# The store of the decoded sequences' value rows: two transfers (112 and 15 partitions) in place of one with 127

## The chip, the cores and the metric

The kernel runs on one core of a Trainium2 chip, as one launch. Its time is the device time of that launch in microseconds. A run of the same program differs from the next by about 1 us.

## What is computed

One decoder layer for 256 prompt tokens and 8 decoded sequences of one token each (264 columns in all). Cut to what matters:

```python
def trunk_layer(x, pe, prm, cache):
    z = rms_norm(x, prm['g_pre_mix']) @ prm['w_in']          # q, k, v and the state-space input u
    attn, k_new, v_new = attn_prompt(...) or attn_sample(..., k_buf, v_buf)
    ssm, s_re, s_im = ssm_mix(u, prm, s0)
    merged = concat([rms_norm(attn, ...), rms_norm(ssm, ...)])
    x = x + rms_norm(merged @ prm['w_out'], ...)
    f = (silu(gu[..., :D_FF]) * gu[..., D_FF:]) @ prm['w_down']    # gu = rms_norm(x) @ w_gate_up
    x = x + rms_norm(f, ...)
    x = x + sigmoid(x @ prm['w_ple_gate']) * (pe @ prm['w_ple_proj'])

def attn_sample(q, k, v, sinks, k_buf, v_buf):
    vals = jnp.concatenate([v_buf, v], axis=1)               # 128 cached rows and the new one
    ...
    return out, keys[:, -WINDOW:], vals[:, -WINDOW:]
```

The last line is the one at hand: for each of the 8 decoded sequences the value cache is given back moved on by one row, that is, the cached rows 1 to 127 and the new row.

## The kernel before

All weights pass TensorE as one stream of blocks (128x128, with 264 columns on the other side). Eight blocks make a unit of 512 KB, which one transfer brings (`raw`, `w_load`, line 332; four buffers). After the first six units, each unit is split into a rounded part by ScalarE (`wh`, `w_high`, line 348) and a rest by VectorE (`wl`, `w_low`, line 356), and TensorE makes three products per block (`acc`, 24 matmuls in a unit). The phases of the stream are `in` (q, k, v, u), `oa` and `os` (the output projection for attention and for the state-space group), `gu`, `dn`, `pg` and `pp`. A unit's buffer can be loaded again once VectorE has made the rest of the unit four before it.

Between the blocks of phase `in`, TensorE also does the attention (`attn`, line 543: scores `s`, transposes `pt`, output `o`) and the state-space group (`ssm_x`: `px`, `ph`, with the table `xtab` that a transfer brings and VectorE's `X` made from it; `ssm_w`: `pw`; `ssm_y`: `py`, then `gy` on ScalarE and its transposes). Each engine works through its instructions in the order in which the program lists them.

That order is not written by hand. `Pace` (line 76) takes each piece of work as a generator and lists the pieces by a rough clock per engine; for a transfer that clock counts half a microsecond on SP, then the bytes (`move`, line 96). What is listed on one engine after another therefore depends on how many transfers there are.

All transfers are issued on SP, one after the other (`dma`, line 289). The value rows' stores stand in `epi_v` (line 505), behind the pieces of VectorE, TensorE and ScalarE on the v columns. The tile `vcd` holds the cached rows: partition r is row r, with 8 sequences of 128 floats (512 bytes) each. The store reads partitions 1 to 127 and writes, for each, 8 runs of 512 bytes that lie 64 KB apart:

```python
        dma(a["o_v"], vnat[:, 1, :])
        dma(a["o_vd"].rearrange("n r d -> r n d")[0:127], vcd[1:128, :, :])
        dma(a["o_vd"][:, 127, :], vself)
        pace.sig("v_out", "sp")
```

`v_out` is waited for in one place, by TensorE's stream on entering phase `os` (line 1529).

Of the kernel before, what the change touches and what calls it, by code (L numbers as in the profile page):

```python
# [16 lines left out]
P = 128  # L17
# [24 lines left out]
def stream_plan():  # L42
    """The order in which the blocks (matrix, output chunk, contraction chunk) pass the tensor engine.
    Eight in a row are a unit, which one transfer brings."""
    b = []

    def chunks(name, ms, nk):
        for m in ms:
            b.extend((name, m, k) for k in range(nk))

    def together(name, ms, nk):
        for k in range(nk):
            b.extend((name, m, k) for m in ms)

    together("in", [0, 4], 16)
    chunks("in", [1, 5, 2, 6, 3, 7, 8, 9] + list(range(10, 18)), 16)
    chunks("oa", range(16), 8)
    chunks("os", range(16), 8)
    chunks("pp", range(8), 2)
    together("gu", EARLY["gu"], 16)  # L60
    chunks("gu", [m for f in range(3, KF) for m in (f, KF + f) if m not in EARLY["gu"]], 16)
    chunks("dn", range(16), KF)
    chunks("pp", range(8, 16), 2)
    together("pg", EARLY["pg"], 16)
    chunks("pg", [m for m in range(16) if m not in EARLY["pg"]], 16)
    return [b[i:i + 8] for i in range(0, len(b), 8)]


# the jobs that share their contraction chunks at the start of these phases
# [6 lines left out]
class Pace:  # L76
    """Writes the program in about the order in which the engines get to it. A task is a generator whose
    segments (an engine, the events that it waits for, the buffers that it takes) are emitted at the
    earliest time that a rough clock per engine allows, the most urgent first."""
# [3 lines left out]
    def __init__(self):  # L83
        self.t = {"pe": 0.0, "dve": 0.0, "act": 0.0, "pool": 0.0, "sp": 0.0}
        self.link = 0.0
        self.table = None
        self.ev = {}
        self.tasks = []
        # when each of the free buffers of a kind came free
        self.res = {n: [0.0] * c for n, c in RES.items()}  # L90
        self.cur = "pe"
# [4 lines left out]
    def move(self, nbytes):  # L96
        """A transfer: the descriptors, then the link."""
        self.t["sp"] += 0.5
        self.link = max(self.link, self.t["sp"] + 0.65) + nbytes / 350e3
# [54 lines left out]
def places(ap):  # L154
    """The elements of a partition that an access touches."""
    i = np.array([ap.offset])
    for stride, n in ap.ap[1:]:
        i = (i[:, None] + stride * np.arange(n)[None]).reshape(-1)
    return i


def interleave(ops, issue=0.1, latency=0.13):
    """An order of the operations (call, operands; the first is written) in which one rarely waits for another."""
    writer, readers, deps = {}, {}, []
    for n, (_, args) in enumerate(ops):
        aps = [x for x in args if hasattr(x, "tensor")]
        d = set()
        for k, ap in enumerate(aps):
            t = ap.tensor.name
            w = writer.setdefault(t, np.full(2048, -1))  # L170
            i = places(ap)
            d.update(w[i].tolist())
            if k == 0:
                for m, j in readers.get(t, []):
                    if np.intersect1d(i, j).size:
                        d.add(m)
        for k, ap in enumerate(aps):
            if k:
                readers.setdefault(ap.tensor.name, []).append((n, places(ap)))
        writer[aps[0].tensor.name][places(aps[0])] = n  # L180
        deps.append(d - {-1, n})
    tail = [0.0] * len(ops)
    for n in reversed(range(len(ops))):
        for m in deps[n]:
            tail[m] = max(tail[m], tail[n] + issue + latency)
    order, end, t = [], {}, 0.0
    left = set(range(len(ops)))
    while left:
        ready = [(max([t] + [end[m] + latency for m in deps[n]]), -tail[n], n) for n in left if deps[n] <= end.keys()]
        t, _, n = min(ready)  # L190
        t += issue
        end[n] = t
        left.remove(n)
        order.append(ops[n][0])
    return order


def build(nc, tc, ctx, a):
# [11 lines left out]
    def deferred(f):  # L210
        """f, or while a list is kept, its call put on the list."""
        def g(*args):
            if later:
                later[-1].append((lambda: f(*args), args))
            else:
                f(*args)
        return g
# [111 lines left out]
    raws, highs, lows = {}, {}, {}  # L329
    at = {"unit": 0}  # L330
# [34 lines left out]
    def warm(func):  # L365
        """Brings an activation function's table in before it is needed."""
        act(spare, epst, func)

# [1 line left out]
    def rstd(ssqs, ones, out, name, evs=()):  # L370
        """out = 1/sqrt(mean + eps) for each column, on every partition; a task's segments. The sum of
        squares comes in one tile or in two, the second of which waits for evs."""
# [25 lines left out]
    def prep_x():  # L398
        """x, and x times the norm's gain."""
        xt = big.tile([P, KD, T], F32, tag="X3", name="xt")  # L400
        XF["t"] = xt
        xr = big.tile([P, KD, T], F32, tag="X1", name="xr")
        XF["r"] = xr
        cuts = [0, 2, 4, 7, 10, 13, 16]
        for c, (k0, k1) in enumerate(zip(cuts, cuts[1:])):
            yield "sp", [f"iss{c - 1}"] if 0 < c < NRAW else []
            dma(xr[:, k0:k1, :], a["x"][:, k0:k1, :])
            pace.sig(f"xl{k0}", "sp")
            if c == 0:
                dma(gains, a["gains"])  # L410
                pace.sig("c_g", "sp")
            for k in range(k0, k1):
                pace.ev[f"xl{k}"] = pace.ev[f"xl{k0}"]
# [91 lines left out]
    def epi_v(ps):  # L505
# [17 lines left out]
        dma(a["o_vd"].rearrange("n r d -> r n d")[0:127], vcd[1:128, :, :])  # L523
# [19 lines left out]
    def attn(g):  # L543
        """Both heads (kv, g): two blocks of queries."""
# [166 lines left out]
    # the imaginary parts, and at last what the products need of the tables: for al -(re + im) and im - re,  # L711
    # for fw, whose conjugate it is that counts, re - im and -(re + im)
# [29 lines left out]
    def exp_poly(out, x):  # L742
        """exp by range reduction and a polynomial."""
# [15 lines left out]
    def cmul(ore, oim, are, aim, bre, bim, t):  # L759
        """(are + i aim)(bre + i bim); t: four scratch tiles."""  # L760
# [7 lines left out]
    def ssm_setup():  # L768
# [69 lines left out]
        # fw[r] = a^(8-r), al[j] = a^(7-j) f  # L838
        n = 1
# [43 lines left out]
        while n < 32:  # L883
            # [0:n] known with n >= 1, the angle of step n in (pc, psn)
# [20 lines left out]
        # the decoded sequences' states, one step on, and their place in SB2  # L905
# [15 lines left out]
    def minus():  # L921
        """The table of sines with its sign turned."""
# [14 lines left out]
    def outer(o, tre, tab, b, bs, e):  # L937
        """o = table (over j) times b (over channels), as complex numbers, from three products."""
# [9 lines left out]
    def ssm_x(e):  # L948
# [43 lines left out]
        # the block's products over time: row (j, c') of step 7 - r is row (j + r, c') of the last step  # L992
# [79 lines left out]
    def ssm_side(e):  # L1072
        """The scan's factors, and the decoded sequences' states."""
# [47 lines left out]
    def ssm_glu(c, first):  # L1121
# [19 lines left out]
        # twice the gated value: (1 + tanh(z / 2)) times the other half  # L1141
# [232 lines left out]
    def epi_pg(ps, m):  # L1374
# [3 lines left out]
        # the last one in two parts, so that the one's way out overlaps the other's arithmetic  # L1378
# [36 lines left out]
    with ExitStack() as order:  # L1415
# [4 lines left out]
        # the tensor engine's clock rises after some microseconds of work: begin before the data is here  # L1420
# [33 lines left out]
        def enter(name):  # L1454
# [6 lines left out]
            if name == "os":  # L1461
                # from here on the program's own order
# [50 lines left out]
        def stream():  # L1513
            phase = None
            for ui, unit in enumerate(UNITS):
                at["unit"] = ui
                if ui == ACCU and ACC0 > 2:
                    # banks for the other work on this engine
# [3 lines left out]
                if unit[0][0] != phase:  # L1522
                    phase = unit[0][0]
                    if phase in ("os", "gu"):
                        # more banks for the stream
# [58 lines left out]
def _constants():  # L1584
# [8 lines left out]
    # rows of the decoded sequences' scores: 32 for a sequence, 16 of them heads  # L1593
# [10 lines left out]
    # the queries' factors: 1/8, and the score's slope put aside  # L1604
# [6 lines left out]
def _layout(x):  # L1611
    """The arrays of setup_inputs() in the layouts that the program loads."""
# [11 lines left out]
    # channel orders: attention chunk g holds (kv, d) of heads (0, g) and (1, g); a chunk of the  # L1624
    # state-space group holds (channel, group)
# [23 lines left out]
    # states: partition (half of the groups, state), free (ri, group of the half)  # L1649
# [10 lines left out]
    def eighths(v):  # L1660
        """[P, ri, groups, n] as [eighth, P, ri groups n]"""
# [66 lines left out]
```

## Time and profile before

| what | value |
|---|---|
| time, median of 3 runs | 1220.92 us (1220.55 to 1221.59) |
| span of the profiled execution | 1217.8 us (its own time is not listed; the runs lie 2.8 to 3.8 us above the span) |
| TensorE (PE) busy | 1181.8 us, 97% of the span |
| VectorE (DVE) busy | 750.6 us, 62% |
| ScalarE (ACT) busy | 590.0 us, 48% |
| GpSimd (POOL) busy | 55.0 us, 5% |
| longest single wait of TensorE | 20.0 us |

Times in the profile are microseconds from the start of the span. A timeline row gives the start, the length, the engine, the program's line, the operation and its tiles, and in brackets how long the engine had stood idle just before and what ended that. PEclk is the clock granted to TensorE as a share of its higher level: 1.00 is 2.4 GHz and 0.50 is 1.2 GHz. SPq is SP's queue, on which transfers are issued; its length is the time that the issuing takes, not that of the transfer.

### The profile page before, as it was taken

Reading aid. Unit: us, or ns where it says so; the run is one execution under the profiler, and the core shown is the slowest. Engines: PE = TensorE matmul, PEld = TensorE weight load, DVE = VectorE, ACT = ScalarE, POOL = GpSimd, SP = SyncE. Lnnn points to the kernel's source line nnn. Section 1 sums busy time; section 2 is a strip of 40 time slices with the busy share of each in tenths; the row PEclk is TensorE's granted clock in tenths of the full one; section 3 lists DMA queues with packets and bytes.
Section 4 is the critical chain, followed back from the end, with each engine's and each line's share of the span. In section 5 each row is a group of like instructions: output and inputs, shape, how many; then the busy total and the mean of one; then the engine's idle time right before and its main releaser. Section 6 shows DMA issues by size and latency. Waiting matters only on the chain.

```text
span 1217.8 us, 23880 instructions
## 1 busy us (share of the span) xinstructions
PE 1181.8 (97%) x9699; PEld 1153.7 (95%) x9699; DVE 750.6 (62%) x1325; ACT 590.0 (48%) x913; POOL 55.0 (5%) x97
## 2 busy tenths in 40 slices
PE   8993999999999999999999999999999999999998
PEld 7893887899999999999999999999999999999998
DVE  8992788967898555555555555555444444446864
ACT  6442887745575444443444444434343444335542
POOL 1111323210000000000000000000000000000000
PEclk9997999999999999999999999999999999999999
DMA  8863554467676666565656555555765666656773
GB/s 269 242 220 112 152 152 154 113 182 254 184 245 201 196 176 188 177 185 179 187 176 188 177 188 176 186 179 186 248 186 177 180 184 177 187 175 194 225 247 117
DMA packets 102184, 228.96 MB, mean 188 GB/s; under 512 B 26969, under 2 KB 50489, under 8 KB 101561
## 3 DMA queue, kind: packets, MB, share of 16 engines
q1 hardware_dynamic: 102073, 227.43, 60.7%
q8 instruction: 76, 1.25, 0.4%
q14 instruction: 35, 0.29, 0.1%
HBM read 214.60 MB, written 12.80 MB: 187 GB/s over the span
## 4 chain that ended last, share of the span: by engine, by line
PE 88%; DVE 6%; DMA 3%; ACT 1%; issue 1%; POOL 0%; SPq 0%; DVEq 0%
PE acc L283 82%; DMA raw<-in_w 2%; PE py L283 1%; DVE wl L222 1%; DVE X L222 1%; DVE rt L222 1%; PE pw L283 1%; PE pt L287 1%; PE s L283 1%; DVE sc L222 0%; ACT s L279 0%; DMA xtab<-in_xtab 0%; DMA xr<-in_x 0%; DVE xl L222 0%; DVE ssq_x L222 0%
## 5 line engine op out<-in xcount | busy, mean ns | idle before, releaser
L222 DVE TENSOR_TENSOR wl<-raw,wh 128x1024 fp32r<-128x1024 f32 x362 | 442.8, 1223 | 321.7 <-PE acc L283 246.8
L279 ACT ACTIVATE wh<-raw 128x1024 fp32r<-128x1024 f32 x362 | 383.9, 1061 | 459.5 <-PE acc L283 432.7
L283 PE MATMUL acc<-hh,wh 128*128 128x264 f32 x1408 | 399.6, 284 | 0.5 <-DVE n_t L236 0.5
L283 PE MATMUL acc<-hh,wl 128*128 128x264 f32 x1408 | 398.6, 283 | 0.0
L283 PE MATMUL acc<-hl,wh 128*128 128x264 f32 x1408 | 398.3, 283 | 0.1
L283 PEld LDWEIGHTS acc<-hh,wh 128*128 128x128 f32 x1408 | 265.2, 188 | 0.7 <-issue 0.7
L283 PEld LDWEIGHTS acc<-hl,wh 128*128 128x128 f32 x1408 | 265.0, 188 | 0.4 <-DVE hl L236 0.3
L283 PEld LDWEIGHTS acc<-hh,wl 128*128 128x128 f32 x1408 | 264.0, 188 | 0.0
L283 PE MATMUL acc<-f,wh 128*128 128x264 f32 x1408 | 256.8, 284 | 0.0
L283 PEld LDWEIGHTS acc<-f,wh 128*128 128x128 f32 x1408 | 217.8, 188 | 0.1
L283 PE MATMUL acc<-f,wl 128*128 128x264 f32 x704 | 199.7, 284 | 0.0
L283 PEld LDWEIGHTS acc<-f,wl 128*128 128x128 f32 x704 | 132.5, 188 | 0.0
L283 PE MATMUL acc<-x2h,wh 128*128 128x264 f32 x256 | 72.7, 285 | 0.0
L283 PE MATMUL acc<-x2h,wl 128*128 128x264 f32 x256 | 72.5, 284 | 0.0
L283 PE MATMUL acc<-xh,wh 128*128 128x264 f32 x240 | 72.1, 300 | 0.0
L283 PE MATMUL acc<-x2l,wh 128*128 128x264 f32 x256 | 71.8, 284 | 0.0
L283 PE MATMUL acc<-xl,wh 128*128 128x264 f32 x240 | 69.7, 290 | 0.4 <-DVE xl L222 0.4
L283 PE MATMUL acc<-xh,wl 128*128 128x264 f32 x240 | 69.3, 289 | 0.7 <-DVE wl L222 0.7
L222 DVE TENSOR_TENSOR uu<-acc,Rf 128x264 f32<-128x264 f32 x44 | 19.0, 432 | 51.0 <-PE acc L283 51.0
L283 PE MATMUL acc<-aops,wh 128*128 128x264 f32 x256 | 48.2, 289 | 0.0
L283 PEld LDWEIGHTS acc<-x2h,wh 128*128 128x128 f32 x256 | 48.1, 188 | 0.0
L283 PEld LDWEIGHTS acc<-x2h,wl 128*128 128x128 f32 x256 | 48.1, 188 | 0.0
(324 smaller groups left out, 1356.1 us busy)
## 6 DMA issues: line engine op xcount, KB each, us to landing
raw<-in_w SPq DMA_DIRECT2D x367, 512.0 KB, 3.6
T<-td SPq DMA_DIRECT2D x8, 512.0 KB, 4.3
xs<-in_x SPq DMA_DIRECT2D x2, 1056.0 KB, 9.4
ppd<-ppt SPq DMA_DIRECT2D x16, 132.0 KB, 3.6
x1d<-oo SPq DMA_DIRECT2D x4, 528.0 KB, 5.6
x<-x1d SPq DMA_DIRECT2D x2, 1056.0 KB, 7.9
ppr<-ppd SPq DMA_DIRECT2D x16, 132.0 KB, 3.7
xtab<-in_xtab SPq DMA_DIRECT2D x8, 256.0 KB, 3.6
```

Of the source, the lines that this page charges most:

```text
L222: V.tensor_tensor(out=out, in0=in0, in1=in1, op=op)
L279: S.activation(out=out, in_=in_, func=func, **kw)
L283: PE.matmul(out, lhsT, rhs, start=start, stop=stop)
L287: PE.transpose(out, in_, ident)
```

## The change

The store of 127 partitions is made as two, of 112 and of 15 partitions, one right after the other in the source. Together they write the same bytes to the same places. Comments are also taken out of the file, so that the lines below the store carry numbers that are higher by three.

```diff
         dma(a["o_v"], vnat[:, 1, :])
-        dma(a["o_vd"].rearrange("n r d -> r n d")[0:127], vcd[1:128, :, :])
+
+        ovd = a["o_vd"].rearrange("n r d -> r n d")
+        dma(ovd[0:112], vcd[1:113, :, :])
+        dma(ovd[112:127], vcd[113:128, :, :])
         dma(a["o_vd"][:, 127, :], vself)
```

Since `Pace` counts one more transfer, it lists some other work in another order as well. On SP, from the store on (`raw` are weight units, `td`, `xtab`, `wg`, `U`, `T` and `cm` belong to the state-space group):

```order
-L294 DMA o_vd<-vcd 127x8x128
+L294 DMA o_vd<-vcd 112x8x128
 L294 DMA raw<-in_w 128x1024
 L294 DMA o_v<-vnat 128x128
+L294 DMA o_vd<-vcd 15x8x128
 L294 DMA o_vd<-vself 8x128
-L294 DMA raw<-in_w 128x1024
+L294 DMA raw<-in_w 128x1024 x2
 L294 DMA td_134<-t_988 128x128
 L294 DMA xtab<-in_xtab 128x512
```

Between the two parts stand a weight unit and the store of the prompt's v rows, and one more weight unit is now issued ahead of `td` and `xtab`.

On VectorE, the rows after the first block of scores (`mx` is the scores' maximum, `nm` and `es` lead to ScalarE's exponentials, `X` needs the table `xtab`, `SB` and `G` are operands of the next `py`). Before:

```order
L222 TENSOR_TENSOR X<-al_109,xtab 128x512
L242 TENSOR_SCALAR nm<-mx 128x4
L222 TENSOR_TENSOR es<-sinks,mx 128x4
L222 TENSOR_TENSOR X<-al_109,xtab 128x512
L222 TENSOR_TENSOR SB_119<-rt_137,rt_138 64x8x32 x2
L222 TENSOR_TENSOR G<-fw_108,cm 128x512 x2
L222 TENSOR_TENSOR wl<-raw,wh 128x1024
L222 TENSOR_TENSOR den<-den,es 128x4
```

With the change, the same stretch on VectorE:

```order
L242 TENSOR_SCALAR nm<-mx 128x4
L222 TENSOR_TENSOR es<-sinks,mx 128x4
L222 TENSOR_TENSOR SB_119<-rt_137,rt_138 64x8x32 x2
L222 TENSOR_TENSOR G<-fw_108,cm 128x512 x2
L222 TENSOR_TENSOR den<-den,es 128x4
L222 TENSOR_TENSOR wl<-raw,wh 128x1024
L578 RECIPROCAL den<-den 128x4
L222 TENSOR_TENSOR G<-G,sc 128x1024
L222 TENSOR_TENSOR X<-al_109,xtab 128x512
```

The two `X` rows have moved behind `nm`, `SB`, `G` and the weight rest. TensorE's order differs only within phase `in`: the transposes of `gy` that follow stand two stream matmuls earlier (after 478 in place of 480), and there are shifts of up to some 10 stream matmuls until 684 of that phase's 768 have been issued; after that its order is the same.

## Rows read from the trace of the kernel before

**Rows 1.** The page's head: the span of the profiled execution.
```profile
span 1217.8 us, 23880 instructions
```

**Rows 2.** Waits of one engine for another between 84 and 121 us: total, times, longest.
```profile
PE py L287 <- ACT gy L279: 20.0, 1, 20.0
```

**Rows 3.** Timeline of VectorE, 91 to 121 us.
```profile
91.63 1.21 DVE L222 TENSOR_TENSOR wl<-raw,wh 128x1024 fp32r<-128x1024 f32 x1
...
115.91 0.69 DVE L222 TENSOR_TENSOR X<-al,xtab 128x512 f32<-128x512 f32 x1 [21.18 <-DMA xtab<-in_xtab]
...
117.50 0.90 DVE L222 TENSOR_TENSOR SB<-rt,rt 64x256 f32<-64x256 f32 x2
118.43 1.29 DVE L222 TENSOR_TENSOR G<-fw,cm 128x512 f32<-128x512 f32 x2
119.65 1.21 DVE L222 TENSOR_TENSOR wl<-raw,wh 128x1024 fp32r<-128x1024 f32 x1
```

**Rows 4.** Timeline of SP, 78 to 113 us: when transfers are issued.
```profile
83.42 0.33 SPq L294 DMA_DIRECT2D o_vd<-vcd  x1
86.53 22.74 SPq L294 DMA_DIRECT2D raw<-in_w  x1
...
111.14 0.37 SPq L294 DMA_DIRECT2D xtab<-in_xtab  x1
```

**Rows 5.** Stretches: length; busy PE, PEld, DVE, ACT, POOL (count); PEclk, DMA share, GB/s.
```profile
90.00:95.00 5.00, 5.00 (x43) 4.01 (x42) 4.33 (x13) 2.34 (x2) 2.22 (x4) 1.00 0.07 22
...
110.00:115.00 5.00, 0.00 (x0) 0.00 (x0) 0.00 (x0) 0.00 (x0) 0.00 (x0) 0.50 0.96 314
...
120.00:130.00 10.00, 9.24 (x59) 8.20 (x60) 8.37 (x21) 7.04 (x14) 3.62 (x3) 0.70 0.45 139
```

**Rows 6.** The transfers' view, 90 to 108 us: packets, then share of 16 engines.
```profile
DMA packets 765, 0.39 MB, mean 22 GB/s; under 512 B 0, under 2 KB 765, under 8 KB 765
...
q1 hardware_dynamic: 765, 0.39, 7.2%
```

**Rows 7.** The page's transfers: issuing queue, count, KB each, median us to landing.
```profile
o_kd<-ktd SPq DMA_DIRECT2D x1, 512.0 KB, 3.8
...
o_v<-vnat SPq DMA_DIRECT2D x1, 64.0 KB, 4.4
```

**Rows 8.** The transfers' view, 22.9 to 23.5 us, in which two 112-row transfers (td<-SB) run.
```profile
DMA packets 211, 0.11 MB, mean 181 GB/s; under 512 B 27, under 2 KB 208, under 8 KB 211
```

**Rows 9.** Timeline of TensorE, 80 to 125 us.
```profile
94.75 2.05 PE L283 MATMUL py<-G,SB 128*128 128x128 f32 x16
...
100.40 0.28 PE L283 MATMUL acc<-xl,wh 128*128 128x264 f32 x1
100.52 0.28 PE L283 MATMUL acc<-xh,wl 128*128 128x264 f32 x1
...
122.33 0.42 PE L283 MATMUL acc<-xh,wh 128*128 128x264 f32 x1
122.55 0.42 PE L283 MATMUL acc<-xl,wh 128*128 128x264 f32 x1
```

**Rows 10.** Timeline of ScalarE, 90 to 122 us.
```profile
118.81 1.28 ACT L279 ACT_TABLE_LOAD   x1
120.10 0.60 ACT L279 ACTIVATE gy<-py 128x512 f32<-128x512 f32 x1
120.60 1.05 ACT L279 ACTIVATE wh<-raw 128x1024 fp32r<-128x1024 f32 x1
```

**Rows 11.** Stretches behind the stall, columns as in rows 5.
```profile
120.00:200.00 80.00, 79.02 (x689) 69.20 (x691) 66.10 (x164) 64.53 (x152) 24.85 (x42) 0.96 0.50 149
200.00:220.00 20.00, 15.07 (x117) 10.49 (x114) 15.89 (x52) 16.65 (x51) 5.12 (x8) 0.91 0.40 119
```

**Rows 12.** Waits of TensorE, 200 to 225 us: total, times, longest.
```profile
PE sd L624 <- POOL q L539: 2.6, 1, 2.6
```

**Rows 13.** TensorE's matmuls of phase os: length min/median/max in ns, first and last start.
```profile
L283 PE MATMUL acc<-sops,wh x256: 278/283/477, 290.7 to 337.0; 128*128 128x264 f32 x128
```

## The prediction

> **What bounds the kernel now.** I read the share of the span first, then the waits, then the stretch in which the longest wait falls, on each engine. TensorE works for 97% of the span of 1217.8 us [rows 1], so nearly everything that is no TensorE time is hidden. What the change can touch is a hole in that. One wait of TensorE stands out: 20.0 us for `gy` from ScalarE [rows 2], after the matmul that starts at 100.52 [rows 9]. ScalarE is not slow there: `gy` takes 0.60 us, behind a table load of 1.28 us [rows 10]. It is late since VectorE is late: VectorE stands idle for 21.18 us until 115.91, when `X` gets its table from the transfer `xtab` [rows 3], and `nm`, which ScalarE's exponentials want, is listed behind `X`. `xtab` is late since SP issues it only at 111.14 [rows 4]. And SP is late since the issue of one weight unit takes 22.74 us from 86.53 on, where the two others in these rows take 0.33 and 0.37 us [rows 4].
>
> What fills the transfers meanwhile? The store `o_vd<-vcd` is issued at 83.42 [rows 4], shortly before. From 90 to 108 us the trace has 765 packets with 0.39 MB [rows 6], which is 512 bytes each, the runs of this store. They come one per 23.5 ns (18 us / 765), at 22 GB/s, and take 7.2% of the 16 engines' time [rows 6], a little over one engine in 16 (6.25%). So one engine carries the store alone: 127 x 8 = 1016 packets x 23.5 ns = 23.9 us. The weight unit behind it has a share on that engine too, and SP is held while that engine's queue doesn't empty. When it has, everything moves at once: 314 GB/s from 110 to 115 us [rows 5].
>
> Compare the store of the k rows: 512 KB in runs of the same 512 bytes, but 128 x 8 of them in place of 127 x 8, landed after 3.8 us [rows 7]. So neither the size nor the packets are at fault, but the 127. The Trainium skill has the rule, in "DMA: Bandwidth & Descriptors", section "Why a DMA increments its semaphore by 16 and not by 1": a transfer goes to the largest number of engines, up to 16, that divides the outermost dimension of both sides; 127 partitions give one engine. By that rule the trace agrees (7.2% of 16 engines), 112 partitions go to 16 engines and 15 to 15.
>
> **What the change does, part by part.** (1) *The part with 112 rows.* 896 packets. If spread over 16 engines they cost 56 x 23.5 ns = 1.3 us of each. The bound on the other side is one engine: 21.1 us. The nearest row is the two transfers of 112 rows between 22.9 and 23.5 us: some 200 packets of 512 bytes in 0.6 us [rows 8], where one engine would move 25. That is many engines, so I take 1.3 us.
>
> (2) *The part with 15 rows.* 120 packets, and no row has such a shape. Spread over 15 engines: 0.2 us; on one engine: 2.8 us. In packets it is nearest to the 112-row transfers, which are spread [rows 8], so I take 0.2 us for the sum, and keep 2.8 us for the range. SP now issues it at about 88 us, between the v store and `vself`; that costs 0.33 us, as the old one did [rows 4], and what is queued behind it, two weight units, has to wait for buffers anyway, the second until VectorE ends a rest at 92.8 [rows 3]. Whoever waits for the whole store is phase `os` at 290.7 us [rows 13], 200 us later: a landing like the 4.4 us of the 64 KB store [rows 7] is hidden, and would be even at 23.9 us. Against cutting a store up the same page, section "Bandwidth", says that transfers under 64 KB are bound by their descriptors; by it the 60 KB part is dear for its size. If its whole landing of 4.4 us were on the path, the sum would be 1204 us and not 1199.7; no row puts it there.
>
> (3) *The stall.* With SP free, the weight unit is issued at 86.53 [rows 4] and those after it as buffers come free, the last of them at 92.8 (91.63 + 1.21 [rows 3]); `td` and `xtab` follow, and `xtab` lands at about 98 (a 512 KB transfer took 3.8 us [rows 7]). In the new order VectorE doesn't want it by then: `nm` and `es` come right behind the scores at 94.73 (115.91 - 21.18). From the end of `X` (115.91 + 0.69 [rows 3]) to the table load at 118.81 [rows 10], `nm` and the exponentials took 2.2 us; so now the load begins at 96.9 and ends at 98.2, and `gy` ends at 98.8. TensorE gets to the transposes of `gy` at 100.5, so that wait of 20.0 us [rows 2] is gone. What is late next is the rest `wl` of the following unit: ScalarE makes `wh` behind `gy` (1.05 us [rows 10]), to 99.9; VectorE `wl` (1.21 us [rows 3]), to 101.1. TensorE wants it after its last matmul and four transposes, five times the 0.12 us between matmuls [rows 9], from 100.5 on: 101.1. New wait: 0 to 0.4 us with the hand-overs; I take 0.4.
>
> (4) *The clock.* In the stall TensorE's clock fell to its lower level, 1.2 GHz: 0.50 from 110 to 115 us and 0.70 on the mean from 120 to 130 [rows 5], so 0.50 until 126.0. Matmuls start 0.22 us apart there, and 0.12 us before the stall [rows 9]. From 120.7 to 126.0 TensorE lost half of 5.3 us, 2.6 us. Without the stall it has no reason to fall there.
>
> (5) *What gives some back.* VectorE had a start on TensorE: it began at 115.91, TensorE at 120.7. In the changed order the two `X` (0.69 us each [rows 3]) come after TensorE has gone on, and TensorE is 2.6 us faster at first: 4.0 us less lead. From 120 to 200 us VectorE works 66.1 of 80 us [rows 11], so 13.9 us are idle, more than enough in sum; but some of it falls where TensorE needs a rest or a `G`. I take 1.0 us, between 0 and 4.0.
>
> (6) *The new order* of the other work in phase `in` runs the same instructions. TensorE is the same from 684 of 768 matmuls on, so the wait at that phase's end (2.6 us for POOL's `q` [rows 12], and PEclk 0.91 over 200 to 220 [rows 11]) stays; bounds: it goes (-2.6 us), or as much is added. I take 0.
>
> Sum on the span: 1217.8 - 20.0 + 0.4 - 2.6 + 1.0 = 1196.6 us. The profiled execution's own time isn't listed; the median of the runs lies 3.1 us above its span, which is outside what the change touches. So 1199.7 us, 21.2 us or 1.7% less.
>
> **Rivals.** *VectorE sets the pace* (18%). If phase `in` hangs on VectorE rather than TensorE, the gain is what VectorE wins: 21.2 us of idle, less the waits that the stall hid. `SB` and `G` overwrite what the running `py` reads until 96.8 [rows 9], some 1.8 us after VectorE is done with `es`, and `wl` waits for `wh` from 99.0 (`SB` and `G` take 0.9 and 1.3 us [rows 3]) to 99.9. 21.2 - 1.8 - 0.9 = 18.5: 1202.4 us. For it: VectorE is full before the store (4.33 of 4.73 us from 90 on [rows 5]). Against it: the 13.9 idle us.
>
> *The 112 rows aren't spread* (3%). Then one engine is held for 21.1 us from about 85, the weight unit lands near 110.5, and only the new order helps, since `gy` no longer hangs on `xtab`: `wh`, `wl` and a hand-over (1.05 + 1.21 + 0.2) put TensorE's next unit at 113, against 120.7: 1213 us. Against it: [rows 8].
>
> *Slower: the new order makes TensorE wait once per block* (3%). Four or five blocks of attention and state-space work remain after the stall. If in each, TensorE met a wait like that of 2.6 us [rows 12], with the clock going down behind it as from 200 to 220 us (0.91 x 20 us: 3.6 us at the lower level, 1.8 us lost [rows 11]), five of them cost 22 us and all is given back: 1221.7 us. Over 3.0 us each it is slower by more than 0.2%. Against it: the order moves rows by 10 matmuls (1.2 us) at most.
>
> **How the numbers follow.** The forecast has 76%, the rivals 18, 3 and 3%; a third of the last lies within 0.2%. The range leaves out the last two and part of the first two: below, 1199.7 less the 1.4 us of (3) and (5) and the 2.6 us of (6), 1195.7, say 1195.5; above, 1199.7 with 3.0 us more in (5) and half of the small part's 2.8 us, 1204.1, say 1204.0, which takes in VectorE's pace. A measurement of this kernel tells 0.2% (2.4 us) from no change. Forecast, VectorE's pace and the unspread store are all faster, 97%; same 1%; slower 2%.
>
> **What would show it.** In the profile of the changed kernel: SP's weight issue at 86.5 takes 0.3 to 0.5 us; no stretch with 22 GB/s; TensorE's wait for `gy` gone; PEclk 1.00 from 80 to 200 us; the start of phase `os` 20 to 24 us earlier. A run of 512-byte packets one per 23.5 ns for 2.8 us would show the small part on one engine. I am wrong if SP's long issue stays, or if waits of TensorE of over 4 us in sum appear between 100 and 185 us.

## The result, and the profile after

| | before | with the change |
|---|---|---|
| median of 4 runs | 1220.74 us (1217.25 to 1221.59) | 1201.3 us (1198.99 to 1204.57) |
| ratio | | 0.9845, 95% interval 0.9819 to 0.9872 |
| profiled execution: span | 1217.8 us [rows 1] | 1201.3 us (its own time 1203.1) |

The change is faster by 1.5%. The forecast was 1199.7 us, the range 1195.5 to 1204.0. No run lies at the median: two took 1198.99 and 1199.5 us, two 1203.1 and 1204.57, and the profile is that of the run with 1203.1. The page of the changed kernel, its head, the engines' shares and the clock over 40 slices (in tenths; 9 is 90% or more):

```profile
span 1201.3 us, 23885 instructions
...
PE 1182.0 (98%) x9699; PEld 1152.1 (96%) x9699; DVE 750.1 (62%) x1325; ACT 589.9 (49%) x913; POOL 55.2 (5%) x97
...
PEclk9999997999999999999999999999999999999999
```

TensorE does the same 1182 us of work in 16.5 us less. The transfers' queue of the changed kernel (start, length of the issue, engine, line, transfer) against [rows 4]:

```profile
83.41 0.42 SPq L294 DMA_DIRECT2D o_vd<-vcd  x1
86.51 0.35 SPq L294 DMA_DIRECT2D raw<-in_w  x1
...
87.39 0.48 SPq L294 DMA_DIRECT2D o_vd<-vcd  x1
...
89.84 3.38 SPq L294 DMA_DIRECT2D raw<-in_w  x2
...
93.79 0.37 SPq L294 DMA_DIRECT2D xtab<-in_xtab  x1
```

The weight unit's issue takes 0.35 us where it took 22.74, and `xtab` goes out 17 us earlier. In the same profile the transfers' view of 83 to 95 us (KB each, us to landing) has both parts landed in ordinary time:

```profile
o_vd<-vcd SPq DMA_DIRECT2D x1, 448.0 KB, 5.7
...
o_vd<-vcd SPq DMA_DIRECT2D x1, 60.0 KB, 4.8
```

VectorE, against [rows 3], and TensorE, against [rows 9], at the place of the old stall:

```profile
94.75 0.17 DVE L242 TENSOR_SCALAR nm<-mx 128x4 f32<-128x4 f32 x1
...
96.89 0.92 DVE L222 TENSOR_TENSOR SB<-rt,rt 64x256 f32<-64x256 f32 x2 [1.91 <-PE py L283]
...
99.49 1.21 DVE L222 TENSOR_TENSOR wl<-raw,wh 128x1024 fp32r<-128x1024 f32 x1
...
101.83 0.68 DVE L222 TENSOR_TENSOR X<-al,xtab 128x512 f32<-128x512 f32 x1
```

```profile
100.26 0.29 PE L283 MATMUL acc<-xh,wh 128*128 128x264 f32 x1
100.38 0.60 PE L287 MATMUL py<-ident,gy 128*128 128x128 f32 x4
100.74 0.37 PE L283 MATMUL acc<-xl,wh 128*128 128x264 f32 x1
```

TensorE goes from stream to transposes to stream without a gap: the wait of 20.0 us [rows 2] is gone, and so is the low clock behind it. What is left lies at the end of phase `in`. Waits of TensorE from 100 to 230 us (total, times, longest), against [rows 12], then the stretches around that end, columns as in [rows 5], then phase `os`, against [rows 13]:

```profile
PE sd L627 <- POOL q L542: 4.1, 1, 4.1
PE pt L287 <- ACT s L279: 1.8, 2, 1.5
...
PE py L287 <- ACT gy L279: 0.3, 1, 0.3
```

```profile
100.00:185.00 85.00, 82.44 (x735) 71.34 (x733) 70.81 (x173) 68.00 (x162) 24.20 (x45) 1.00 0.53 159
...
180.00:200.00 20.00, 13.54 (x96) 9.18 (x95) 14.26 (x47) 14.55 (x47) 3.98 (x6) 0.82 0.37 102
200.00:210.00 10.00, 10.00 (x76) 6.81 (x76) 4.90 (x13) 6.41 (x20) 1.45 (x4) 0.68 0.15 42
```

```profile
L283 PE MATMUL acc<-sops,wh x256: 278/283/477, 274.3 to 320.7; 128*128 128x264 f32 x128
```

Phase `os` begins 16.4 us earlier (290.7 to 274.3), and the span is 16.5 us shorter: all of the difference is made in phase `in`, and none after it. But at the end of `in` the wait for GpSimd's `q` has grown from 2.6 to 4.1 us, and the clock behind it is at 1.2 GHz for 7.2 us (0.18 x 20 / 0.5) and then 6.4 us, 13.6 in all, against 3.6 us before.

Why `q` is later can be read on SP, GpSimd and VectorE. VectorE makes `q` behind `sc`, `sc` needs GpSimd's `bs`, and `bs` needs another `xtab`. The kernel before, SP and VectorE:

```profile
198.87 0.36 SPq L294 DMA_DIRECT2D xtab<-in_xtab  x1
199.68 0.33 SPq L294 DMA_DIRECT2D ys<-yt  x1
```

```profile
202.81 0.77 DVE L222 TENSOR_TENSOR sc<-al_re,bs 128x512 f32<-128x512 f32 x1 [0.21 <-POOL bs L270]
```

With the change, SP, GpSimd and VectorE:

```profile
177.83 0.33 SPq L294 DMA_DIRECT2D ys<-yt  x1
178.27 0.36 SPq L294 DMA_DIRECT2D xtab<-in_xtab  x1
```

```profile
182.70 0.32 POOL L270 TENSOR_TENSOR bs<-xtab 128x64 f32<-128x64 f32 x1 [3.47 <-DMA xtab<-in_xtab]
```

```profile
183.05 0.77 DVE L222 TENSOR_TENSOR sc<-al_re,bs 128x512 f32<-128x512 f32 x1 [1.72 <-POOL bs L270]
```

In the new order SP issues `xtab` behind `ys` and not ahead of it. It took 4.4 us to land, and VectorE stood for 1.72 us in place of 0.21: 1.5 us more, by which TensorE's wait grew.

### The profile page after: what moved, and what is told of

Same layout as the page of the kernel before. It is cut to its first block, busy times and chain, and to the rows that moved or that the text cites. A ratio compares the mean times of both kernels' runs of the same rounds, so it can differ in the third digit from the quotient of the medians.

```text
span 1201.3 us, 23885 instructions
## 1 busy us (share of the span) xinstructions
PE 1182.0 (98%) x9699; PEld 1152.1 (96%) x9699; DVE 750.1 (62%) x1325; ACT 589.9 (49%) x913; POOL 55.2 (5%) x97
## 4 chain that ended last, share of the span: by engine, by line
PE 88%; DVE 7%; ACT 2%; DMA 1%; issue 1%; SPq 0%; POOL 0%; DVEq 0%
PE acc L283 83%; PE py L283 1%; DVE wl L222 1%; DVE X L222 1%; DMA xtab<-in_xtab 1%; ACT s L279 1%; DVE rt L222 1%; PE pw L283 0%; DMA xr<-in_x 0%; DVE sc L222 0%; PE s L283 0%; DVE ssq_x L222 0%; DVE xl L222 0%; DVE s L565 0%; PE pt L287 0%
```

## The experiments

Two things changed at once: the store is spread, and the rest of phase `in` is listed in another order. The runs take them apart, ask what decides the number of engines, and try to get back what the end of the phase loses. All were timed against the kernel before on the same chip (median 1219 to 1221 us there). Each result is the median, the range and the ratio to the kernel before with its 95% interval. Where runs of different experiments are compared, some were on different chips.

**The store of 112 rows alone, in the order of before.** The order listing of this kernel is that of the kernel before on every engine, since the number of transfers is the same.

```diff
-        dma(a["o_vd"].rearrange("n r d -> r n d")[0:127], vcd[1:128, :, :])
+        dma(a["o_vd"].rearrange("n r d -> r n d")[0:112], vcd[1:113, :, :])
```

> One store of 112 partitions with the order of before on every engine; the last 15 of the 127 rows are left out. It separates the spreading of the store from the new order. If the spreading alone removes the stall: SP's weight issue at 86.5 us takes under 1 us, xtab is issued at about 91 us and lands at about 95, VectorE's X waits 0 to 2 us for it, TensorE waits at most 2 us for gy, time 1197 to 1203 us. If the new order carries a part of the gain (X before nm in the old one holds ScalarE up): X waits 3 to 6 us, TensorE 2 to 5 us for gy, time 1203 to 1207 us. If the transfer is not spread: as before, 1218 to 1221 us.

Measured: 1197.77 us (1196.48 to 1200.83), ratio 0.9821 (0.9803 to 0.9838). From its profile, SP's and VectorE's rows at the place of the stall, a wait of TensorE, and phase `os`:

```profile
86.58 0.35 SPq L294 DMA_DIRECT2D raw<-in_w  x1
...
91.15 0.37 SPq L294 DMA_DIRECT2D xtab<-in_xtab  x1
```

```profile
95.31 0.69 DVE L222 TENSOR_TENSOR X<-al,xtab 128x512 f32<-128x512 f32 x1 [0.52 <-DMA xtab<-in_xtab]
```

```profile
PE sd L624 <- POOL q L539: 2.6, 1, 2.6
```

```profile
L283 PE MATMUL acc<-sops,wh x256: 278/283/477, 268.0 to 314.4; 128*128 128x264 f32 x128
```

VectorE's wait for `xtab` fell from 21.18 to 0.52 us, TensorE waited for `gy` nowhere, and phase `os` began 22.7 us earlier. The spreading alone removes the stall; the new order is not needed for it.

**Parts of 113 and 14.** The order of the change on every engine, as in the next run: `Pace`'s clock is still given the bytes of 112 and 15 rows, and the transfers are issued past the helper `dma`.

```diff
-        dma(ovd[0:112], vcd[1:113, :, :])
-        dma(ovd[112:127], vcd[113:128, :, :])
+        pace.move(4.0 * 112 * 1024)
+        SP.dma_start(out=ovd[0:113], in_=vcd[1:114, :, :])
+        pace.move(4.0 * 15 * 1024)
+        SP.dma_start(out=ovd[113:127], in_=vcd[114:128, :, :])
```

> Two parts as in the change, but of 113 and 14 partitions; the order on every engine is that of the change. 113 has no divisor from 2 to 16. If the engine count follows the outermost count: the first part runs on one engine, 904 packets x 23.5 ns = 21.2 us at 22 GB/s, SP's weight issue at 86.5 us takes about 20 us; the new order lets TensorE go on with one unit, so a stall of 10 to 18 us and 1210 to 1218 us. If two transfers are enough, whatever their counts: no stall, 1199 to 1204 us.

Measured: 1213.98 us (1212.86 to 1217.39), ratio 0.9957 (0.9941 to 0.9972). From its profile the packets from 90 to 103 us, SP's issue, and TensorE's longest wait:

```profile
DMA packets 552, 0.28 MB, mean 22 GB/s; under 512 B 0, under 2 KB 552, under 8 KB 552
...
q1 hardware_dynamic: 552, 0.28, 7.2%
```

```profile
86.48 19.27 SPq L294 DMA_DIRECT2D raw<-in_w  x1
```

```profile
PE pt L287 <- ACT s L279: 11.2, 4, 9.2
```

One row more in the first part brings the stall back: 552 packets in 13 us are again one per 23.5 ns. So it is the count 113 and not the number of transfers. It also shows what the new order is worth when a store is not spread: TensorE got on to 102 us and then stood for 9.2 us, so that the kernel is some 5 us faster than before (ratio 0.9957), near the 1213 us worked out for the rival of a store that isn't spread.

**Parts of 80 and 47.**

```diff
-        dma(ovd[0:112], vcd[1:113, :, :])
-        dma(ovd[112:127], vcd[113:128, :, :])
+        pace.move(4.0 * 112 * 1024)
+        SP.dma_start(out=ovd[0:80], in_=vcd[1:81, :, :])
+        pace.move(4.0 * 15 * 1024)
+        SP.dma_start(out=ovd[80:127], in_=vcd[81:128, :, :])
```

> Two parts of 80 and 47 partitions, the order of the change. 80 goes to 16 engines, 47 (no divisor from 2 to 16) to one: 376 packets x 23.5 ns = 8.8 us. It asks how long one engine may be held before TensorE notices. If four weight buffers cover it: SP's weight issues are held for some microseconds, TensorE waits no more than in the change, 1199 to 1205 us. If a held engine costs its length: some 8 us more than the change, 1207 to 1211 us.

Measured: 1203.76 us (1200.48 to 1203.98), ratio 0.986 (0.9843 to 0.9876). SP's queue in its profile:

```profile
87.23 0.33 SPq L528 DMA_DIRECT2D o_vd<-vcd  x1
87.65 8.74 SPq L294 DMA_DIRECT2D o_vd<-vself  x1
...
96.49 0.84 SPq L294 DMA_DIRECT2D raw<-in_w  x2
```

By their packets the 47 rows held one engine for 8.8 us. SP was held for 8.74 us, at the next transfer, which is the 4 KB of `vself`: what is held is the transfer issued next, a unit of 512 KB behind 127 and 113 rows, 4 KB here. TensorE hardly noticed. It waited 0.9 us for VectorE's `q` behind the late `xtab`, and a tenth or two more elsewhere. A held engine cost nothing that shows while there was other work in hand: 8.8 us are covered here, and of 21.2 us (parts of 113 and 14) about half showed (1214 us against 1203 for the change's repeats below).

**Parts of 64 and 63.** Edited like the two before.

```diff
+        pace.move(4.0 * 112 * 1024)
+        SP.dma_start(out=ovd[0:64], in_=vcd[1:65, :, :])
+        pace.move(4.0 * 15 * 1024)
+        SP.dma_start(out=ovd[64:127], in_=vcd[65:128, :, :])
```

> Two parts of 64 and 63 partitions, the order of the change. 63 is odd but 9 divides it. If the number of engines is a divisor of the outermost count: the 63 rows go to 9 engines, 504 / 9 = 56 packets or 1.3 us of each; no stretch at 22 GB/s, as the change, 1199 to 1204 us. If any count that 16 does not divide goes to one engine: 504 packets x 23.5 ns = 11.8 us on it, SP held for some 11 us, TensorE waiting 2 to 5 us, 1203 to 1209 us.

Measured: 1198.98 us (1197.34 to 1203.6), ratio 0.9838 (0.9812 to 0.9864). SP was not held (0.51 us for the 63 rows' issue, the weight units at 90.04). An odd count is no fault by itself. TensorE's wait for `q` is 2.9 us in its profile, and three of the four runs have a mean clock of 0.999 (1197.34 to 1199.53 us). That these are nine engines and not some other number was not read from the trace, which has no engine's name.

These counts agree with the rule of the Trainium skill that the prediction cited ("DMA: Bandwidth & Descriptors", "Why a DMA increments its semaphore by 16 and not by 1"): 127, 113 and 47 have no divisor up to 16 but one, and were moved at 22 GB/s or held SP for nearly their packets x 23.5 ns (22.74, 19.27 and 8.74 us against 23.9, 21.2 and 8.8); 112, 80 and 63 have one and were not.

**All 128 partitions in one store, with one row too many.** The output takes 129 rows a sequence, and the host takes the last 128.

```diff
-        dma(a["o_vd"].rearrange("n r d -> r n d")[0:127], vcd[1:128, :, :])
-        dma(a["o_vd"][:, 127, :], vself)
+        dma(a["o_vd"].rearrange("n r d -> r n d")[0:128], vcd)
+        dma(a["o_vd"][:, 128, :], vself)
```

> One store of all 128 partitions of the tile into an output of 129 rows a sequence (the new row goes to the last), from which the host takes rows 1 to 128: a whole result in one transfer with an outermost count of 128, and the order of before on every engine. If the order of before with a spread store is the better one, as the store of 112 partitions alone showed: no stall, TensorE waits 2.6 us at the end of phase in, 1196 to 1200 us, some 3 to 4 us under the change run beside it. If that kernel was faster only for its 15 missing rows: 1200 to 1204 us.

Measured: 1199.6 us (1197.42 to 1200.65), ratio 0.9835 (0.9813 to 0.9857); the change beside it 1203.24 (below). As expected: whole, in the order of before, and faster than the change by some 3 us on the median, so the 15 missing rows were not what made the store of 112 fast. The parts of 64 and 63, on the same chip and in the order of the change, were as fast on the median (1198.98 us); what the order costs is therefore not settled by this pair.

**Parts of 96 and 16.**

```diff
+        dma(ovd[0:96], vcd[1:97, :, :])
+        dma(ovd[96:112], vcd[97:113, :, :])
```

> Two parts of 96 and 16 partitions, 112 in all, the last 15 rows left out, the order of the change on every engine. It differs from the single store of 112 in the number of transfers and the order that follows from it, and from the change in the 15 rows alone. If the order is what the change lost: as the change, 1199 to 1204 us, with a wait of about 4 us at the end of phase in. If the small part of 15 rows is what it lost: 1196 to 1199 us.

Measured: 1203.06 us (1199.39 to 1204.66), ratio 0.9861 (0.9837 to 0.9886). As slow as the change, without the part of 15 rows, and slower than the single store of the same 112 rows (on another chip) by 5 us on the median, by 2 to 3 us at neighbouring mean clocks (1203.05 at 0.994 against 1200.83 at 0.995, 1199.39 at 0.997 against 1196.48 and 1196.9 at 0.999). So the small part costs nothing that can be measured, and the order costs something. The wait, though, was expected at about 4 us and is 3.0: `xtab`, behind `ys` here too, landed in 3.2 us (64 and 63: 3.2 us as well, wait 2.9; the change: 4.4, 4.1 and 3.9 us, wait 4.1, 3.9 and 3.6). The wait follows the landing of `xtab`. No run put `xtab` ahead of `ys` by itself.

**The change again, twice,** for more runs and their mean granted clock.

> The change itself, beside the others on one chip, for more runs of it with their granted clock. Both theories: 1198.5 to 1204.5 us; runs with a mean clock of 0.999 at 1199, those with 0.993 or 0.994 at 1203 to 1205.

> The change beside these two, for the comparison on one chip: 1199 to 1205 us.

Measured: 1203.24 us (1199.31 to 1204.41), ratio 0.9862 (0.9837 to 0.9886); and 1202.81 us (1199.39 to 1203.24), ratio 0.9854 (0.9829 to 0.9879). With the first four there are 14 runs of the change. Six had a mean clock of 0.996 to 0.999 and took 1198.99 to 1200.74 us; eight had 0.993 or 0.994 and took 1202.81 to 1204.57. Nothing lies between. The profile of the first repeat is of a run with a mean clock of 0.999. Its stretches at the end of phase `in`:

```profile
180.00:200.00 20.00, 13.79 (x101) 9.45 (x99) 15.10 (x49) 15.47 (x49) 4.24 (x7) 0.91 0.36 100
200.00:210.00 10.00, 10.00 (x102) 8.33 (x101) 7.35 (x19) 8.42 (x22) 2.98 (x6) 1.00 0.53 139
```

The wait is nearly the same (3.9 us for `q`, against 4.1), but TensorE's clock is at 1.2 GHz for 3.6 us and not 13.6. The spans differ by 3.8 us (1197.5 and 1201.3), and so do the starts of phase `os` (270.5 and 274.3). What differs between these two executions of the changed kernel is the clock at the end of phase `in`; of the runs without a profile the mean clock says the same. The kernel before scatters in the same way: of its 36 runs beside the experiments, 15 have a mean clock of 0.990 and took 1216.51 to 1218.51 us, 17 have 0.986 or 0.987 and took 1220.03 to 1223.2, and four lie between. So runs of one program differ by several microseconds and not by about 1, and the change is worth some 18 us in either group (1199.4 against 1217.5, 1203.2 against 1221.3, medians). The store of 129 rows has the same two cases, but lower: 1197.42 us at 0.999, 1199.12 to 1200.65 at 0.995 and 0.996.

**GpSimd's copies of q on VectorE.** If the wait for `q` is GpSimd's fault, take the work from it.

```diff
-        yield "pool"
         for h in range(2):
             r = slice(64 * h, 64 * h + 64)
-            pace.use("pool", 0.1)
-            G.tensor_copy(out=q32[r, :, 8 * h + g], in_=q[r, 256:264])
+            V.tensor_copy(out=q32[r, :, 8 * h + g], in_=q[r, 256:264])
+        yield "pool"
+        pace.use("pool", 0.2)
```

> The change, with the 16 small copies of q for the decoded sequences on VectorE in place of GpSimd. At the end of phase in, TensorE waits 4.1 us for these copies in the changed kernel (2.6 us before), and the clock is lower for 13.7 us behind that. If GpSimd's 2.3 us for the last pair is what is late: the wait falls to about 2 us, the clock falls less, 1195 to 1199 us. If VectorE's own lateness (X waiting for xtab) is what counts, or its 16 more copies cost as much: 1199 to 1204 us.

Measured: 1202.79 us (1200.43 to 1204.39), ratio 0.9852 (0.9833 to 0.987). The first theory missed: the wait fell from 4.1 to 3.4 us only. GpSimd's 2.3 us were replaced, but `q` itself came later from VectorE, which stood for 1.9 us for `bs` and so for `xtab`. That is the second theory, VectorE's own lateness.

**Ten matmuls on constants in the wait.** On the store of 129 rows:

```diff
         sd = [bank([P, 129], f"sd{i}") for i in range(2)]
+        for _ in range(10):
+            mm(sd[0][:, 0:P], onesd, onesd, 0.22)
```

> The store of 129 rows, with ten matmuls on constants put ahead of sd at the end of phase in, where TensorE otherwise waits 2.6 us (they write the bank that sd then overwrites). It tests whether the idle time there brings the clock down. If it does: less or no time at the lower clock behind 185 us, and the runs come together at 1196 to 1198 us. If the clock falls whatever stands there: 1197 to 1202 us, as without them.

Measured: 1195.72 us (1195.37 to 1196.12), ratio 0.9807 (0.9784 to 0.9829), beside the change at 1202.81 us. This is the fastest of all, and its four runs lie within 0.8 us. TensorE (the profile counts two instructions for each of the ten) at the end of the phase, and the stretches:

```profile
182.83 2.40 PE L283 MATMUL sd<-onesd 128*128 128x128 f32 x20
185.62 0.65 PE L626 MATMUL sd<-ktd,q 128*32 128x129 f32 x16 [0.39 <-POOL q L539]
```

```profile
180.00:200.00 20.00, 18.22 (x175) 14.49 (x173) 18.61 (x55) 18.60 (x57) 6.95 (x11) 1.00 0.44 128
200.00:210.00 10.00, 8.74 (x71) 7.82 (x70) 9.56 (x25) 8.41 (x20) 1.84 (x5) 1.00 0.36 101
```

The clock stays at 2.4 GHz through the end of the phase, in this profile and by the means (0.999 to 1.000) in all four runs. Against the same store without them (on another chip), the best run gained 2.1 us and the worst 4.5. Not all of it is the clock: the ten matmuls also change the order behind `sd` (the transposes `pt` now come ahead of the scores in one piece), and that part was not tried by itself.

**The last scores ahead of sd.** The same wait filled with work that has to be done anyway, again on the store of 129 rows.

```diff
+        pace.sig(f"q{g}", "dve")
         yield "pool"
...
         pace.sig(f"qd{g}", "pool")
-        pace.sig(f"q{g}", "pool")
```

> The store of 129 rows, with the last heads' scores listed as ready once VectorE has q, and not once GpSimd has copied it: TensorE does 1.9 us of scores in the wait ahead of sd, the same work. If the wait counts by its length and for the clock: sd's wait 0 to 1 us, 1194 to 1198 us. If something else is late behind it (the probabilities, the products of the last block): waits of the same sum elsewhere, 1197 to 1202 us.

Measured: 1202.71 us (1201.02 to 1203.91), ratio 0.9863 (0.9841 to 0.9884). A miss. The wait for `sd` is 0.4 us, but the new order put a product before its operand was ready. TensorE's waits in its profile from 185 to 215 us:

```profile
PE py L283 <- DVE SB L222: 4.4, 1, 4.4
PE ps_a L283 <- DVE decT L222: 1.5, 1, 1.5
```

**Sixteen matmuls on constants, on the change.**

```diff
         sd = [bank([P, 129], f"sd{i}") for i in range(2)]
+        for _ in range(16):
+            mm(sd[0][:, 0:P], onesd, onesd, 0.22)
```

> The change with 16 matmuls on constants ahead of sd, where it waits 3.6 to 4.1 us. If what the change falls short of the filled store of 129 rows (1195.7 us) is the clock behind this wait alone: 1195.5 to 1197 us, mean clock 0.999 to 1.000. If its order costs something that a filled wait does not give back (a later q, small waits between 100 and 185 us): 1197 to 1199.5 us with the same clock.

Measured: 1205.23 us (1203.01 to 1205.57), ratio 0.9872 (0.9846 to 0.9899). Neither theory: slower than the change. The wait ahead of `sd` was filled (0.5 us left), but the order behind it moved the last head's scores some 7 us back, to 196.65, and the wait came back there, with the clock:

```profile
PE pt L287 <- ACT s L279: 3.1, 1, 3.1
PE ps_a L283 <- DVE aops L222: 2.0, 1, 2.0
...
```

```profile
200.00:220.00 20.00, 14.50 (x103) 10.68 (x99) 11.80 (x35) 14.86 (x40) 3.59 (x6) 0.74 0.25 70
```

So it doesn't tell how much of the change's own shortfall is the clock. It shows that the order at the end of this phase, which no line of the source sets, can give back all that a filled wait gains.

## Why the prediction was right, and where a term was off

The mechanism of the stall was right at every step; that the median came out so near the forecast is in part luck (below). One engine carried the 127 rows; the 112 rows were spread; SP, VectorE and ScalarE came free in that order; `gy` was ready before TensorE wanted it (98.8 us expected, and 98.82 by ScalarE's row: 98.22 and 0.60).

- *(1), (2) The two parts.* 112 rows landed in 5.7 us, 15 in 4.8 us. The 15 rows cost nothing (parts of 96 and 16 were as slow), so the 2.8 us kept for them in the range were not needed.
- *(3) The stall.* 20.0 us, gone. The 0.4 us of a new wait for the weight rest did not come: `wl` began at 99.49 and not at 99.9, as ScalarE made `wh` from 98.72 on.
- *(4) The clock.* 1.00 from 85 to 185 us, so the stall's low clock is gone. Two of the signs named did not come, both for the end of the phase: the clock was not 1.00 up to 200 us (0.82 from 180 to 200), and phase `os` began 16.4 us earlier and not 20 to 24. In the first repeat it began 20.2 us earlier (270.5).
- *(5) What gives some back.* From 100 to 185 us TensorE was idle for 2.6 of 85 us, and 1.2 of these are the start of the wait for `q` (from 183.8); the other 1.4 us are small waits, for `gy`, `XT` and `ws` (0.3 to 0.4 us each) and others. The kernel before had 0.5 us of these in the like stretch (120.7 to 205 us), so some 0.8 us are new, where (3) and (5) had put down 1.4 together.
- *(6) The new order* is the term that was mis-sized. It was put at 0, since TensorE's order is the same from 684 of 768 matmuls on, with 2.6 us either way. The wait at the phase's end became 3.6 to 4.1 us: that the same instructions stand in the same order on TensorE says nothing about when their operands come, and on SP `xtab` had moved behind `ys`. At a low mean clock the order costs 3 to 4 us (1203.2 to 1204.4 at 0.993 and 0.994 against 1199.1 to 1200.7 at 0.995 and 0.996 for the store of 129 rows, beside each other). At a high one it costs 0 to 2 us (1199.3 against a single run with 1197.4; but the parts of 64 and 63 took 1197.3 to 1199.5 in the same order). The clock behind the wait, low for 13.6 us and not 3.6 in eight of 14 runs by their mean clock, can't be laid to the order alone, since the runs of the kernel before divide as well.
- *What lies around the span* was put at 3.1 us, the median less the span of one profile whose own time wasn't listed. In every run listed with its span it is 1.8 us. So the profiled execution was some 1.3 us below the median of before, and the sum for such an execution was 1196.6 + 1.8 = 1198.4 us. That error and (6) go against each other, and the median of 1201.3 us, 1.6 above the forecast, lies between two groups in which all 14 runs fall: that part is luck. Like for like the sum holds better. In the first repeat, whose clock was low for 3.6 us at the phase's end as in the trace of before, the small waits were 0.9 us longer than there and the wait for `q` 1.3: 1217.8 - 20.0 - 2.6 + 0.9 + 1.3 = 1197.4 us, and its span is 1197.5.
- *The rivals.* VectorE's pace (1202.4 us) names a time near the median for another reason: the wait that decides is one, at the end of the phase, where VectorE stands for a transfer; it is not VectorE's work over the whole phase. The store that isn't spread was run as 113 rows and came out at 1214, against the 1213 worked out.

Two sentences ahead of the prediction are wrong. One is that runs differ by about 1 us: those of the kernel before range from 1216.5 to 1223.2 us. The other is that `Pace` changes the order since it counts one more transfer. Listings of the change with the two parts counted as one have the order of the change, and those of the single store counted as two have the order of before. In these listings it is the number of transfer instructions itself that decides. So the order seems to be made behind `Pace`, by the framework's own scheduling, which ends at the line `manual_schedule`; that was not traced further. The prediction's numbers don't rest on it.

## What to carry to other kernels

Look for transfers whose outermost count has no divisor from 2 to 16 (127, 113 and 47 here): the sign is not the slow transfer itself, which nobody may wait for, but a later transfer whose issue takes tens of microseconds and a stretch at 22 GB/s. A row more (128), or parts of 112 and 15 or of 64 and 63 rows, removed it here; one transfer over a rounded count has the advantage that it leaves the order of the rest alone. And when an edit changes the number of instructions, compare the order far behind it as well, on the queue of transfers and not on TensorE alone, and look at the clock behind each wait of TensorE of a few microseconds.

## What the runs showed that was not expected

The same wait of TensorE has two outcomes. After 3.9 us of waiting for `q` the clock was at 1.2 GHz for 3.6 us in one execution of the change, and after 4.1 us for 13.6 us in another; with 2.6 us of waiting, the stores of 112 and of 129 rows show both cases too (mean clock 0.999 and 0.995). The 14 runs of the change fall into two groups some 4 us apart, and most runs of the kernel before do so too; a median of four runs, or one profile, says little about differences of 2 or 3 us here. Ten matmuls on constants in that wait brought the store of 129 rows together at 1195.4 to 1196.1 us.

And SP is not held by the transfer that sits on one engine, whose issue took 0.32 or 0.33 us, but by the one after it, even if that has 4 KB (8.74 us).
